# A new table of priority shifts for a list-scheduled six-stage decoder kernel

## The chip, the cores and the metric

The kernel runs on one core of one Trainium2 chip. The metric is device time in microseconds (us) from the first to the last instruction with what lies around them, the median of repeated runs.

## What is computed

Two layers of a decoder over 256 tokens of width 1024 in float32. Each layer is a feed-forward block, a mixer and a second feed-forward block, each followed by a layer norm of a weighted sum:

```python
def reference(x, positions, ...):
    h = x
    for layer in range(2):
        h = layer_norm(ALPHA * h + 0.5 * swiglu(h, ffn_w_in[layer, 0], ffn_w_out[layer, 0]), ...)
        if layer % 2 == 0:
            mix = hybrid_mixer(h, ...)       # gated delta rule + state-space scan
        else:
            mix = nsa_mixer(h, positions, ...)   # compressed, selected and window attention
        h = layer_norm(ALPHA * h + mix, ...)
        h = layer_norm(ALPHA * h + 0.5 * swiglu(h, ffn_w_in[layer, 1], ffn_w_out[layer, 1]), ...)
    return h

def swiglu(x, w_in, w_out):              # w_in 1024 x 5632, w_out 2816 x 1024
    gate, up = split(x @ w_in, 2)
    return (silu(gate) * up) @ w_out
```

The gated delta rule of the hybrid mixer solves a triangular system in each chunk of 64 tokens, for eight heads.

## The kernel before

The stages of the run are numbered 0 to 5: feed-forward, hybrid mixer, feed-forward, feed-forward, attention mixer, feed-forward. All weights are streamed from memory once.

**Products in three parts.** A float32 weight tile of 128 x 1024 lands in a buffer named `raw`. ScalarE (or VectorE) copies it, rounded, into `whi`; VectorE subtracts the two and keeps the rest in `wlo`. Activations are split in the same way (`x`, `g` or `gh` and `gl`, `fhi` and `flo` by their place). A product is then three matmuls: high by high, low by high, high by low. In most of a feed-forward stage, seven products of blocks stand for eight (`wide` in the code), which needs sums of weight blocks (`raw<-raw,raw` on VectorE), some of them made by accumulating transfers from GpSimd's queue.

**Turning.** The gated result of a chunk has to be transposed before the second product. In some chunks TensorE does that; in others ScalarE writes 16-bit `words`, SyncE issues two DMA transposes into `turned`, and ScalarE puts the result together (`gT`).

**Buffers.** Tiles of 128 x 1024 come from 44 slots shared by named streams (raw tiles, split tiles and so on), each with a quota. A stream's tiles are granted in program order. PSUM has eight banks under three names, `ps`, `mp` and `acc`.

**What sets the order.** The Python program first only records operations, 8,350 in all, each with its place in the program as its priority, and then runs a list scheduler (`Plan.order`). It walks in modelled time, and at every step takes, for the engine that can start soonest, the ready operation with the smallest priority. Costs, latencies, two DMA queues and the slots are modelled. The instructions are emitted in the order that comes out; each engine then works through its own list strictly in that order, waiting on semaphores for what isn't ready. SyncE's list holds most loads, the DMA transposes and the stores; GpSimd's list holds the accumulating loads.

**The table.** Before the scheduler runs, `SHIFTS` is applied: for each stage and engine it holds runs of (count, shift), counted over that engine's operations of the stage in program order. Operations past the last run get none:

```python
for eng, runs in shifts.items():
    mine = iter([op for op in ops if op.eng == eng])
    for count, shift in runs:
        for op in islice(mine, count):
            op.prio += shift
```

A shift of -500 lets an operation go ahead of ready operations that stand up to 500 places earlier. It can't make an operation ready sooner.

All instructions are recorded by one helper line (L707 in the profile), so tiles' names tell them apart.

Of the kernel before, what the change touches and what calls it, by code (L numbers as in the profile page):

```python
# [49 lines left out]

SHIFTS = {
    0: {
        "tensor": [(73, 35), (42, 0), (3, -303), (2, 677), (60, 285), (4, 0), (6, 272), (80, 180), (61, 0), (1, 89), (2, 0), (5, 76), (12, 0),
            (5, 185), (9, 128), (22, 0), (46, -94), (1, 272), (8, 0), (1, 429), (45, 247), (112, 0), (6, -69), (1, 1116), (147, 0), (19, -333)],
        "vector": [(26, 0), (11, 505), (3, 0), (1, 981), (9, 332), (2, 1157), (16, 37), (8, 0), (1, 36), (2, 12), (2, 0), (3, 40), (2, -49),
            (2, -314), (6, -28), (5, -335), (8, 0), (6, -130), (1, 239), (20, 0), (7, -457), (15, 90), (9, 68), (28, 27)],
        "scalar": [(51, 1316), (49, 299), (32, 0), (4, -174), (7, -332)],
        "sync": [(21, 512), (4, 0), (2, 1305), (42, -829), (1, -837)],
    },
    1: {  # L60
        "tensor": [(78, 0), (5, 102), (45, 13), (1, 126), (57, 0), (5, 165), (56, -1495), (2, 137), (46, 0), (1, 116), (27, 0), (2, 316), (4, 0),
# [4 lines left out]
        "vector": [(61, 79), (16, -214), (2, -277), (20, 0), (22, -481), (36, 0), (3, 243), (2, 0), (8, -1712), (6, 0), (3, 122), (3, 0), (2, -781),  # L66
            (1, 785), (7, 0), (5, -96), (13, 0), (3, -348), (12, 0), (5, 955), (6, 0), (2, -2056), (7, 82), (2, -244), (4, 0), (7, -2770), (2, -226),
            (7, -312), (14, -616), (13, 0), (2, -170), (3, 235), (31, 0), (1, 104), (3, 0), (45, -78), (11, -721)],
        "scalar": [(36, 0), (6, -475), (29, 0), (27, -175), (2, 128), (3, 0), (1, -552), (4, 68), (13, 0), (2, -580), (18, 0), (2, 1271), (31, 0),
            (26, -544), (51, 0), (2, 137), (15, 0), (11, 358), (8, -97), (2, 2193), (7, -854)],  # L70
        "gpsimd": [(3, 0), (2, -233)],
        "sync": [(40, 0), (1, -488), (4, 0), (4, -608)],
    },
    2: {
        "tensor": [(2, 151), (39, 28), (11, 0), (6, -515), (27, 0), (14, -125), (19, 120), (157, 30), (177, 0), (5, -87), (4, 0), (9, -961), (4, 0),
            (33, -162), (4, -408), (5, 100), (80, 0), (27, 151), (7, 0), (2, 167), (11, 0), (1, -218), (2, -189), (2, -136), (1, -210), (7, -310),
            (10, -171), (6, -305), (5, -340), (13, 61), (13, -822), (1, 0), (37, -386), (1, 98), (22, 0), (14, 68)],
        "vector": [(10, -109), (7, -190), (4, 103)],
        "scalar": [(12, 0), (3, -357), (78, 1148), (35, 0), (1, -118)],
    },  # L80
    3: {
        "tensor": [(36, 0), (4, -133), (4, 0), (6, -109), (1, 778), (37, 0), (2, 738), (31, 505), (107, 0), (7, 177), (18, 0), (23, 487), (5, 0),
            (2, 1186), (1, 1660), (23, 1445), (19, -442), (12, 41), (14, -333), (2, 0), (1, -306), (5, -732), (3, 0), (4, 101), (123, 0), (6, -597),
            (170, 0), (62, -115), (28, -595)],
        "vector": [(40, 239), (10, 0), (11, 402), (4, 1341), (5, 0), (1, 554), (110, 0), (6, -268)],
        "scalar": [(66, 735), (32, 0), (10, -856)],
        "sync": [(43, 0), (2, -897)],
    },
    4: {
        "tensor": [(1, 435), (72, 0), (8, 132), (1, 358), (38, 0), (19, 167), (1, 272), (10, 0), (7, 192), (1, 427), (14, -543), (8, 518), (68, 75),  # L90
            (60, 0), (7, -103), (5, 42), (70, 0), (122, 124), (3, 0), (4, -102), (3, 0), (1, -524), (10, -43), (3, -211), (17, 0), (8, -186),
            (2, -392), (2, 0), (36, -364), (1, -98), (2, -410), (9, 21), (39, 0), (10, 303), (17, 239)],
        "vector": [(68, 0), (3, -666), (71, 0), (9, -229), (3, 0), (25, -315)],
        "scalar": [(124, 98), (11, 0), (41, 123), (4, 0), (9, -109), (14, 5), (8, 0), (2, -850), (2, -72)],
        "sync": [(1, 31)],
    },
    5: {
        "tensor": [(51, 140), (26, 0), (2, 803), (90, 0), (23, 974), (14, 0), (17, 113), (5, 0), (89, 892), (47, 0), (4, 3124), (3, 3103), (1, 4070),
            (24, 937), (42, -1815), (2, 1390), (18, 0), (8, 322), (1, 0), (34, 288), (19, -2444), (14, -1291), (3, 0), (15, -1630), (12, -161),
            (2, 0), (125, -150), (5, 324), (4, 299), (18, 187), (21, 0), (14, 332), (4, 0), (28, 346)],  # L100
        "vector": [(12, 382), (19, 0), (4, 193), (20, 0), (18, 1029), (12, 0), (2, 1342), (6, 645), (12, 0), (79, -160)],
        "scalar": [(71, 853), (58, 53)],
        "sync": [(42, 0), (10, -188), (18, 98)],
    },
}

# [2469 lines left out]
```

## Time and profile before

| what | value |
|---|---|
| median of 3 runs | 1067.26 us (1066.71 to 1068.01) |
| profiled execution | 1069.88 us |
| its span | 1068.2 us |
| mean granted TensorE clock | 0.995 |
| TensorE matmuls busy | 1051.2 us, 98% |
| VectorE busy | 1004.6 us, 94% |
| ScalarE busy | 765.7 us, 72% |
| moved from memory | 221.30 MB, 208 GB/s over the span |

The span is the time from the first to the last instruction of the profiled execution; the time of that execution is measured around it. In rows, PE is TensorE's matmuls and PEld its weight loads, DVE is VectorE, ACT ScalarE, POOL GpSimd, and SPq SyncE's queue of transfers. Busy time counts an engine as busy from an instruction's start to its end; matmuls overlap in the pipeline and their ends are modelled.

### The profile page before, as it was taken

Reading aid. Unit: us, or ns where it says so; the run is one execution under the profiler, and the core shown is the slowest. Engines: PE = TensorE matmul, PEld = TensorE weight load, DVE = VectorE, ACT = ScalarE, POOL = GpSimd, SP = SyncE. Lnnn points to the kernel's source line nnn. Section 1 sums busy time; section 2 is a strip of 40 time slices with the busy share of each in tenths; the row PEclk is TensorE's granted clock in tenths of the full one; section 3 lists DMA queues with packets and bytes.
Section 4 is the critical chain, followed back from the end, with each engine's and each line's share of the span. In section 5 each row is a group of like instructions: output and inputs, shape, how many; then the busy total and the mean of one; then the engine's idle time right before and its main releaser. Section 6 shows DMA issues by size and latency. Waiting matters only on the chain.

```text
span 1068.2 us, 15981 instructions
## 1 busy us (share of the span) xinstructions
PE 1051.2 (98%) x5714; PEld 869.8 (81%) x5714; DVE 1004.6 (94%) x1417; ACT 765.7 (72%) x1154; POOL 88.5 (8%) x130
## 2 busy tenths in 40 slices
PE   9999999999999999999999999999999999999987
PEld 6877888899889888888888888888887778887866
DVE  7999999799989999998999999999988989999977
ACT  7677966479856977776876678788475867787771
POOL 1001000001000221100000200000011110000100
PEclk9999999999989999999999999999999999999999
DMA  9899996753772799889879846998563373687981
GB/s 316 277 286 263 257 322 196 200 144 102 180 200 84 209 272 333 238 239 263 273 228 318 222 158 211 263 260 267 169 204 132 112 234 80 198 249 199 274 271 40
DMA packets 178586, 233.52 MB, mean 219 GB/s; under 512 B 46973, under 2 KB 108106, under 8 KB 178506
## 3 DMA queue, kind: packets, MB, share of 16 engines
q1 hardware_dynamic: 169258, 214.67, 63.7%
q0 software_dynamic: 9248, 17.83, 9.9%
q8 instruction: 45, 0.74, 0.3%
q14 instruction: 35, 0.29, 0.1%
HBM read 221.30 MB, written 1.07 MB: 208 GB/s over the span
## 4 chain that ended last, share of the span: by engine, by line
PE 84%; DVE 7%; DMA 4%; ACT 2%; issue 1%; POOL 1%; SPq 0%; DVEq 0%; POOLq 0%; ACTq 0%
PE acc L707 33%; PE ps L707 26%; PE mp L707 25%; DMA raw<-in_ffn_w_in_dram 2%; DVE arena L707 1%; DMA raw<-in_ffn_w_out_dram 1%; DVE h L707 1%; DVE wlo L707 1%; DVE cv L707 1%; POOL arena L707 1%; DVE o L707 1%; ACT P L707 1%; DMA raw<-in_nsa_cmp_w_dram 1%; DVE F L707 0%; ACT sw L707 0%
## 5 line engine op out<-in xcount | busy, mean ns | idle before, releaser
L707 DVE TENSOR_TENSOR wlo<-raw,whi 128x1024 fp32r<-128x1024 f32 (+2 forms) x447 | 523.1, 1205 | 13.8 <-ACT whi L707 13.4
L707 ACT ACTIVATE whi<-raw 128x1024 fp32r<-128x1024 f32 (+2 forms) x426 | 424.9, 1046 | 66.9 <-DVE raw L707 37.8
L707 PE MATMUL ps<-whi,x 128*128 128x512 f32 (+1 forms) x544 | 146.0, 385 | 0.0
L707 DVE TENSOR_TENSOR raw<-raw,raw 128x1024 f32<-128x1024 f32 x94 | 112.1, 1216 | 2.6 <-DMA raw<-in_ffn_w_in_dram 2.1
L707 PEld LDWEIGHTS ps<-whi,x 128*128 128x128 f32 x544 | 97.6, 188 | 18.5 <-ACT vg L707 0.4
L707 PE MATMUL ps<-x,whi 128*128 128x512 f32 (+2 forms) x464 | 106.3, 344 | 0.5 <-ACT cv L707 0.5
L707 PE MATMUL acc<-wlo,gh 128*128 128x512 f32 x253 | 99.1, 392 | 1.7 <-DVE wlo L707 1.7
L707 PE MATMUL acc<-whi,gh 128*128 128x512 f32 x253 | 97.5, 393 | 1.5 <-ACT whi L707 1.5
L707 PE MATMUL acc<-whi,gl 128*128 128x512 f32 x253 | 97.7, 392 | 0.0
L707 PEld LDWEIGHTS ps<-x,whi 128*128 128x128 f32 (+1 forms) x464 | 78.2, 189 | 10.1 <-ACT cv L707 1.3
L707 PE MATMUL acc<-whi,x 128*128 128x512 f32 x256 | 82.2, 404 | 1.1 <-ACT whi L707 1.1
L707 PE MATMUL mp<-whi,x 128*128 128x512 f32 x288 | 78.9, 392 | 0.0
L707 PE MATMUL ps<-wlo,x 128*128 128x512 f32 (+1 forms) x272 | 78.2, 382 | 0.0
L707 PE MATMUL mp<-whi,fhi 128*128 128x512 f32 x192 | 75.0, 392 | 0.0
L707 PE MATMUL mp<-whi,flo 128*128 128x512 f32 x192 | 74.7, 390 | 0.0
L707 POOL DMA_DIRECT2D raw<-in_ffn_w_in_dram x34 | 41.1, 1209 | 382.3 <-DMA raw<-in_ffn_w_in_dram 142.1
L707 PE MATMUL ps<-x,wlo 128*128 128x256 f32 (+1 forms) x344 | 66.0, 284 | 0.0
L707 PE MATMUL acc<-whi,g 128*128 128x512 f32 x192 | 63.8, 391 | 0.0
L707 PEld LDWEIGHTS mp<-whi,x 128*128 128x128 f32 x288 | 53.1, 188 | 12.1 <-ACT vg L707 1.0
L707 PE MATMUL mp<-wlo,fhi 128*128 128x512 f32 x192 | 60.0, 392 | 1.8 <-DVE wlo L707 1.8
L707 PEld LDWEIGHTS acc<-wlo,gh 128*128 128x128 f32 x253 | 47.5, 188 | 12.7 <-DVE wlo L707 2.7
L707 PEld LDWEIGHTS acc<-whi,x 128*128 128x128 f32 x256 | 47.3, 188 | 12.5 <-ACT whi L707 1.7
(323 smaller groups left out, 1852.0 us busy)
## 6 DMA issues: line engine op xcount, KB each, us to landing
raw<-in_ffn_w_in_dram SPq DMA_DIRECT2D x162, 512.0 KB, 6.5
raw<-in_ffn_w_out_dram SPq DMA_DIRECT2D x88, 512.0 KB, 6.1
raw<-in_hyb_w_in_dram SPq DMA_DIRECT2D x44, 512.0 KB, 5.6
raw<-in_ffn_w_in_dram POOLq DMA_DIRECT2D x34, 512.0 KB, 9.5
raw<-in_ffn_w_in_dram SPq DMA_DIRECT2D x52, 256.0 KB, 4.5
raw<-in_hyb_w_out_dram SPq DMA_DIRECT2D x16, 512.0 KB, 4.4
raw<-in_nsa_w_in_dram SPq DMA_DIRECT2D x10, 512.0 KB, 5.1
raw<-in_nsa_cmp_w_dram SPq DMA_DIRECT2D x8, 512.0 KB, 4.9
```

Of the source, the lines that this page charges most:

```text
L707: r = getattr(getattr(nc, eng), fn)(*[res(a) for a in args], **{k: res(a) for k, a in kw.items()})
```

## The change

The table `SHIFTS` is replaced as a whole; nothing else is edited. By the description that came with it, the old and the new table are the outcome of a search, and the new one judged each order by the mean of replays in which transfers are issued when slots are free and land at scattered times. Runs that differ can be counted from the two tables and the program's list: of the tensor instructions, 479 of 812 in stage 0 get another shift, 916 of 1,375 in stage 1, 549 of 800 in stage 2, 568 of 792 in stage 3, 412 of 687 in stage 4 and 649 of 785 in stage 5. The last 18 SyncE entries of stage 5 are 12 loads of output weights, the two rows of the layer norm and the four stores; the entries 59 and 64 of that list are DMA transposes.

The diff, cut to the stages 3 and 5 (the others are rewritten in the same way):

```diff
--- before.py
+++ after.py
@@ -50,57 +50,60 @@
...
     3: {
-        "tensor": [(36, 0), (4, -133), (4, 0), (6, -109), (1, 778), (37, 0), (2, 738), (31, 505), (107, 0), (7, 177), (18, 0), (23, 487), (5, 0),
-            (2, 1186), (1, 1660), (23, 1445), (19, -442), (12, 41), (14, -333), (2, 0), (1, -306), (5, -732), (3, 0), (4, 101), (123, 0), (6, -597),
-            (170, 0), (62, -115), (28, -595)],
-        "vector": [(40, 239), (10, 0), (11, 402), (4, 1341), (5, 0), (1, 554), (110, 0), (6, -268)],
-        "scalar": [(66, 735), (32, 0), (10, -856)],
-        "sync": [(43, 0), (2, -897)],
+        "tensor": [(58, 217), (9, 0), (1, 99), (42, 0), (3, -97), (67, 0), (4, -120), (48, 667), (3, 0), (5, 851), (21, 0), (1, 372), (74, 89),
+            (24, 0), (84, 1255), (71, 0), (3, 388), (11, 0), (1, 531), (27, 0), (3, 397), (3, 0), (1, 405), (117, -629), (15, -906), (13, 0),
+            (3, -677), (13, 97), (29, 0), (11, 122), (6, 0), (12, 198)],
+        "vector": [(11, 237), (6, 0), (43, 175), (2, 816), (4, 727), (9, 637), (19, 0), (4, 1258), (18, 0), (1, 578), (4, 0), (6, 202), (33, 0),
+            (1, 77)],
+        "scalar": [(66, 487), (23, 0), (4, 446), (3, 162), (3, 0), (2, -331), (12, 0), (20, 658)],
     },
...
     5: {
-        "tensor": [(51, 140), (26, 0), (2, 803), (90, 0), (23, 974), (14, 0), (17, 113), (5, 0), (89, 892), (47, 0), (4, 3124), (3, 3103), (1, 4070),
-            (24, 937), (42, -1815), (2, 1390), (18, 0), (8, 322), (1, 0), (34, 288), (19, -2444), (14, -1291), (3, 0), (15, -1630), (12, -161),
-            (2, 0), (125, -150), (5, 324), (4, 299), (18, 187), (21, 0), (14, 332), (4, 0), (28, 346)],
-        "vector": [(12, 382), (19, 0), (4, 193), (20, 0), (18, 1029), (12, 0), (2, 1342), (6, 645), (12, 0), (79, -160)],
-        "scalar": [(71, 853), (58, 53)],
-        "sync": [(42, 0), (10, -188), (18, 98)],
+        "tensor": [(2, 197), (25, -123), (15, 0), (1, 769), (2, 0), (6, 64), (1, 0), (9, 299), (16, 0), (8, 1127), (38, -515), (45, 0), (2, 1282),
+            (16, -364), (1, 514), (19, 92), (81, 0), (1, 322), (61, 0), (3, 260), (5, 0), (2, 1081), (3, 0), (4, 3690), (16, 396), (10, 100),
+            (4, 4396), (29, 0), (14, 312), (2, -1131), (34, 0), (22, -910), (1, 65), (20, -455), (46, 120), (95, 0), (3, -282), (4, 0), (17, -146),
+            (36, 0), (15, -113), (2, 0), (1, -92)],
+        "vector": [(6, 580), (3, 0), (3, 163), (11, 0), (6, 65), (2, 0), (5, 114), (2, -89), (8, -768), (19, -95), (1, 732), (22, 404), (43, 0),
+            (8, -74), (10, 0), (3, -251), (5, 0), (27, -124)],
+        "scalar": [(8, 43), (9, -32), (46, 865), (30, 305), (25, 0), (4, 471), (2, 0), (1, 496)],
+        "sync": [(70, 0), (18, -517)],
     },
 }
```

## Rows read from the trace of the kernel before

**Rows 1.** From the profile page of the whole run: the span, busy time of the engines with their instruction counts, the busy share of the DMA engines in 40 slices (tenths), the shares of the chain that ended last, and the issues of output-weight loads with the median us from issue to landing.

```profile
span 1068.2 us, 15981 instructions
...
PE 1051.2 (98%) x5714; PEld 869.8 (81%) x5714; DVE 1004.6 (94%) x1417; ACT 765.7 (72%) x1154; POOL 88.5 (8%) x130
...
DMA  9899996753772799889879846998563373687981
...
PE 84%; DVE 7%; DMA 4%; ACT 2%; issue 1%; POOL 1%; SPq 0%; DVEq 0%; POOLq 0%; ACTq 0%
...
raw<-in_ffn_w_out_dram SPq DMA_DIRECT2D x88, 512.0 KB, 6.1
```

**Rows 2.** Stretches of 25 us, three from the middle feed-forward stages and one from the hybrid mixer: the stretch, its length, then busy time and instructions of each engine, the granted TensorE clock, the DMA share and GB/s.

```profile
500.00:525.00 25.00, 25.00 (x111) 20.51 (x110) 24.75 (x23) 19.74 (x22) 0.00 (x0) 1.00 0.86 243
650.00:675.00 25.00, 25.00 (x111) 20.63 (x110) 24.97 (x25) 21.55 (x25) 2.40 (x2) 1.00 0.83 268
700.00:725.00 25.00, 25.00 (x111) 20.53 (x110) 25.00 (x25) 20.35 (x24) 0.00 (x0) 1.00 0.94 271
300.00:325.00 25.00, 24.41 (x437) 22.42 (x436) 21.14 (x37) 11.22 (x17) 0.31 (x1) 0.86 0.50 156
```

**Rows 3.** The whole run cut into stages, with the same columns: the opening, the rest of the first feed-forward stage, the hybrid mixer, two feed-forward stages, the attention mixer, the last feed-forward stage, and the tail.

```profile
0.00:25.00 25.00, 22.84 (x94) 16.96 (x95) 17.02 (x25) 17.86 (x25) 4.61 (x25) 1.00 0.93 311
25.00:184.00 159.00, 157.62 (x718) 128.20 (x717) 155.08 (x167) 115.95 (x145) 10.78 (x9) 1.00 0.88 267
184.00:412.00 228.00, 226.73 (x1714) 198.96 (x1714) 211.30 (x429) 167.58 (x278) 20.19 (x28) 0.99 0.66 185
412.00:587.00 175.00, 175.00 (x805) 144.43 (x804) 170.55 (x187) 128.00 (x158) 13.82 (x13) 1.00 0.87 265
587.00:761.00 174.00, 174.00 (x796) 143.68 (x795) 173.40 (x208) 127.48 (x160) 9.95 (x10) 1.00 0.78 226
761.00:881.00 120.00, 118.78 (x792) 94.08 (x791) 106.90 (x213) 85.11 (x245) 16.16 (x36) 1.00 0.53 169
881.00:1050.00 169.00, 165.40 (x749) 134.35 (x749) 157.63 (x169) 123.72 (x150) 11.15 (x10) 1.00 0.72 201
1050.00:1068.20 18.20, 10.84 (x57) 9.16 (x55) 12.71 (x26) 0.00 (x0) 1.85 (x2) 0.86 0.16 59
```

**Rows 4.** TensorE's matmul side, who waited for whom over the whole run: total us, times, longest us.

```profile
PE acc L707 <- ACT whi L707: 2.6, 2, 1.5
PE mp L707 <- DVE wlo L707: 1.8, 2, 1.4
PE acc L707 <- DVE wlo L707: 1.7, 2, 0.9
```

**Rows 5.** TensorE's weight loads in order of time, those that sat idle before them (in brackets: idle us and what ended it), in the first and the last feed-forward stage: start us, us, engine, operation, out<-in, tile, count.

```profile
76.64 0.30 PEld L707 LDWEIGHTS mp<-wlo,fhi 128*128 128x128 f32 x2 [1.80 <-DVE wlo L707]
...
982.48 0.30 PEld L707 LDWEIGHTS mp<-wlo,fhi 128*128 128x128 f32 x2 [0.82 <-DVE wlo L707]
...
1021.72 0.19 PEld L707 LDWEIGHTS acc<-whi,gh 128*128 128x128 f32 x1 [1.95 <-ACT whi L707]
1022.98 0.19 PEld L707 LDWEIGHTS acc<-wlo,gh 128*128 128x128 f32 x1 [1.07 <-DVE wlo L707]
...
1029.71 0.19 PEld L707 LDWEIGHTS acc<-wlo,gh 128*128 128x128 f32 x1 [1.26 <-DVE wlo L707]
```

**Rows 6.** The chain that ended last, between 1008 and 1031 us: start us, us, what.

```profile
1012.76 10.53 DMA raw<-in_ffn_w_out_dram
...
1023.38 1.06 ACT whi L707
...
1028.44 1.23 DVE wlo L707
```

**Rows 7.** SyncE's queue between 1000 and 1026 us in order of time (start us, us over which the issues stretch, out<-in, count), then the same loads in a window that ends at 1013 us, and, as the last line, the duration of a transpose's issue over the whole run (ns, least/median/most).

```profile
1002.30 9.73 SPq L707 DMA_TRANSPOSE turned<-words  x2
1012.13 11.56 SPq L707 DMA_DIRECT2D raw<-in_ffn_w_out_dram  x10
...
1012.13 1.05 SPq L707 DMA_DIRECT2D raw<-in_ffn_w_out_dram  x2
...
L707 SPq DMA_TRANSPOSE turned<-words x32: 1232/1284/6093, 95.8 to 1008.5; - x32
```

**Rows 8.** Stretches around that place, columns as in rows 2 (the last two numbers are the DMA share and GB/s).

```profile
985.00:995.00 10.00, 10.00 (x46) 8.14 (x44) 9.97 (x9) 7.78 (x10) 1.20 (x1) 1.00 0.75 220
995.00:1002.30 7.30, 7.30 (x33) 5.83 (x32) 6.98 (x8) 6.38 (x8) 1.20 (x1) 1.00 1.04 257
1002.30:1012.10 9.80, 9.80 (x44) 8.01 (x44) 8.10 (x10) 6.30 (x7) 1.19 (x1) 1.00 1.09 321
1012.10:1023.30 11.20, 8.94 (x37) 6.56 (x37) 8.04 (x8) 5.28 (x5) 1.20 (x1) 1.00 1.23 227
```

**Rows 9.** The two conversions of a weight tile, all of their kind in the run: busy us, mean ns of one, idle time before them and what ended it.

```profile
L707 DVE TENSOR_TENSOR wlo<-raw,whi 128x1024 fp32r<-128x1024 f32 x436 | 514.6, 1215 | 13.0 <-ACT whi L707 12.6
L707 ACT ACTIVATE whi<-raw 128x1024 fp32r<-128x1024 f32 x416 | 417.9, 1053 | 61.0 <-DVE raw L707 37.8 <-DMA raw<-in_ffn_w_out_dram 5.4 <-DVE h L707 2.8
```

More of the change, by code (lines that the diff above doesn't have):

```diff
@@ L52 @@
     0: {
[L53 to L56, printed above, removed]
@@ L57 @@
-        "scalar": [(51, 1316), (49, 299), (32, 0), (4, -174), (7, -332)],
-        "sync": [(21, 512), (4, 0), (2, 1305), (42, -829), (1, -837)],
-    },
-    1: {
-        "tensor": [(78, 0), (5, 102), (45, 13), (1, 126), (57, 0), (5, 165), (56, -1495), (2, 137), (46, 0), (1, 116), (27, 0), (2, 316), (4, 0),
[4 rows of a table removed]
[L66 to L72, printed above, removed]
-    },
@@ L74 @@
-    2: {
[L75 to L79, printed above, removed]
-    },
@@ L89 @@
-    4: {
[L90 to L95, printed above, removed]
-    },
@@ L97 @@
-    5: {
-        "tensor": [(51, 140), (26, 0), (2, 803), (90, 0), (23, 974), (14, 0), (17, 113), (5, 0), (89, 892), (47, 0), (4, 3124), (3, 3103), (1, 4070),
-            (24, 937), (42, -1815), (2, 1390), (18, 0), (8, 322), (1, 0), (34, 288), (19, -2444), (14, -1291), (3, 0), (15, -1630), (12, -161),
-            (2, 0), (125, -150), (5, 324), (4, 299), (18, 187), (21, 0), (14, 332), (4, 0), (28, 346)],
-        "vector": [(12, 382), (19, 0), (4, 193), (20, 0), (18, 1029), (12, 0), (2, 1342), (6, 645), (12, 0), (79, -160)],
-        "scalar": [(71, 853), (58, 53)],
-        "sync": [(42, 0), (10, -188), (18, 98)],
+        "tensor": [(33, 160), (108, 0), (3, 677), (34, 0), (6, 297), (119, 81), (45, 0), (6, 674), (148, 0), (1, 496), (13, -172), (10, 272), (4, 0),
+            (7, 184), (2, 109), (29, 0), (4, 213), (2, 0), (10, 174), (2, 610), (15, 299), (4, 1187), (15, 382)],
@@ new lines @@
+        "vector": [(33, 0), (2, 157), (26, 0), (4, -268), (14, 337), (3, 0), (3, 569), (27, 137), (1, 118), (1, 188), (2, 0), (1, 274), (14, -404),
+            (2, 1222), (4, 0), (3, -1554), (1, -77), (2, -377)],
+        "scalar": [(130, 0), (1, 345), (11, 0), (1, 417)],
+        "sync": [(22, 73), (2, 63), (57, 57)],
+    },
+    1: {
+        "tensor": [(78, 0), (8, 108), (37, 0), (12, 87), (21, -126), (3, -45), (1, 0), (1, 57), (42, -4), (15, -78), (28, 28), (73, 0), (8, 274),
[5 rows of a table added]
+        "vector": [(77, 395), (7, 0), (11, 206), (1, 356), (71, 0), (3, -1139), (4, 0), (1, -443), (2, 62), (2, 462), (36, 0), (2, 257), (19, 146),
+            (10, 0), (1, 302), (5, -254), (20, 0), (9, -570), (12, 0), (1, -373), (4, -179), (3, 748), (1, -764), (21, 0), (2, -275), (22, 0),
+            (1, -191), (26, 0), (16, -3263)],
+        "scalar": [(103, 30), (21, 0), (40, 820), (90, 0), (1, -415), (2, 0), (11, -187), (17, 597)],
+        "gpsimd": [(7, 0), (1, 460)],
+    },
@@ new lines @@
+    2: {
+        "tensor": [(53, 0), (84, -29), (7, 325), (51, 0), (1, 267), (6, 0), (11, 149), (27, -808), (15, 57), (4, -369), (1, 0), (1, 298), (2, 177),
+            (28, 0), (37, -178), (40, 0), (1, 181), (1, 0), (1, 2273), (3, 2155), (2, 0), (2, 3273), (4, 118), (3, 2378), (107, 0), (26, 560),
+            (30, 0), (7, -157), (28, 0), (1, 1365), (6, 0), (2, 1935), (14, 0), (2, 1483), (48, 224), (64, 0), (9, -3469), (18, 0), (7, -571)],
+        "vector": [(27, 0), (3, 505), (33, -105), (9, -389), (46, 0), (18, -97), (4, -201), (1, 0), (2, -173), (2, -2013), (1, -172), (12, -1939)],
+        "scalar": [(101, 346), (7, 0), (2, 308)],
+    },
@@ new lines @@
+    4: {
+        "tensor": [(2, 381), (75, 0), (1, 134), (61, 0), (1, 245), (4, 0), (6, -264), (10, 115), (12, -208), (20, 48), (116, 0), (11, -736), (68, 0),
+            (4, 166), (21, 0), (19, 287), (20, 0), (6, -303), (1, 164), (19, 0), (1, 249), (2, 329), (7, 474), (12, 364), (13, 201), (12, 0),
+            (1, 286), (7, 0), (1, 367), (46, -238), (10, 0), (9, 228), (2, 0), (2, 686), (1, 356), (3, 0), (1, 292), (33, 0), (9, -596), (1, 1067),
+            (14, 0), (5, 761), (18, 150)],
+        "vector": [(68, 0), (10, -775), (14, 0), (8, 114), (67, 0), (12, 146)],
+        "scalar": [(98, 0), (12, -231), (17, 286), (9, 0), (1, 264), (18, 0), (6, 423), (20, 0), (2, 782)],
+        "gpsimd": [(64, 0), (7, -209)],
+        "sync": [(1, 107), (1, 75)],
+    },
```

9 rows, old and new, of the table SHIFTS are left out of this document.

## The prediction

> **What bounds the kernel.** I read the profile page first. TensorE is busy for 1051.2 of 1068.2 us, VectorE for 1004.6, and 84% of the chain that ended last is TensorE [rows 1]. The reader is to see that nothing but the matmul stream sets the length of most of the run, and that VectorE is close behind it. Whether that stream has slack inside is the next question, because busy time of pipelined matmuls can hide a slow pace. So I took 25 us stretches from the two middle feed-forward stages: each holds 111 matmuls and has no idle time [rows 2], that is 25.00 / 111 = 225 ns from one 128x512 product to the next. The same 111 comes back in three stretches 200 us apart, so this is the engine's own pace, and an order can't improve on it.
>
> The Trainium skill would have me look elsewhere: its page Perfetto Trace Analysis, section Identifying the Most-Contended Engine, says that matmul busy time is a poor measure of headroom and that the busy share of weight loads is a better one. That share is 81% here, which read as headroom would be about 200 us, against the 17 us that TensorE's idle time gives. The repeated pace of 111 products speaks for the smaller number, and I use it alone.
>
> The third view cuts the run by stage [rows 3]. Subtracting the busy from the length of each stretch gives TensorE's idle time: 2.16 us in the opening, 1.38 in the rest of the first feed-forward stage, 1.27 in the hybrid mixer, none in the two middle feed-forward stages (349 us together), 1.22 in the attention mixer, 3.60 in the last feed-forward stage up to 1050 us, and 7.36 in the tail. The sum is 16.99, which is all of 1068.2 - 1051.22. A new order of ready work can't shorten the opening (the first bytes have to come) nor much of the tail (two layer norms follow the last products). What an order can win is 1.38 + 1.27 + 1.22 + 3.60 = 7.5 us of idle time. Beside it stands a stretch in the hybrid mixer in which the granted clock falls to 0.86 in the mean over 25 us, after 437 small products [rows 2]; at half clock for 0.14 x 25 x 2 = 7 us, it costs about 3.5 us. The most that a perfect order could give back is therefore about 11 us, 1% of the run.
>
> **What the waits are.** TensorE's own waits are few and nearly all are for split weights: 2.6, 1.8 and 1.7 us [rows 4]. In time order they are a wait of 1.80 us on the weight side at 76.6 us, one of 0.82 at 982.5, and three of 1.95, 1.07 and 1.26 us between 1021.7 and 1029.7 [rows 5]. The last three have one cause, and the chain shows it: a transfer of output weights issued at 1012.76 lands 10.53 us later, its high part takes 1.06 us, a low part 1.23 [rows 6]. Such transfers land in 6.1 us in the median [rows 1]. It was late because the queue of SyncE was held for 9.73 us by two DMA transposes from 1002.30 on; ten output-weight loads were issued behind them, in 11.56 us [rows 7]. A transpose holds its queue for 1.28 us in the median and for 6.09 at most [rows 7]. The ten loads then meet a full memory path: the DMA share is 1.09 during the transposes and 1.23 in the stretch after [rows 8].
>
> **What the change does.** It adds, removes and resizes no instruction. It changes the number that is added to an operation's place in the program before the list scheduler picks among ready operations. Counted over the two tables, 3,573 of the 5,251 tensor instructions get another shift, at least 59% in every stage. So the order within an engine is drawn anew nearly everywhere, bounded by the dependences and by the buffers, which are still granted in program order. Direct cost in instructions: nothing. What moves is who waits.
>
> *Last feed-forward stage.* The last 18 SyncE entries go from no shift to -517: they are the 12 last output-weight loads, the two norm rows and the four stores. The transposes ahead of them lose their shift of +98 and stay at their place, some 820 and 860. So where a slot is free, these loads now sort ahead of the two transposes that held the queue, which they did not before. If they go first, the 10.53 us landing starts up to 9.7 us earlier and the three waits go: their idle time on TensorE is the stage's 3.60 less the wait at 982.5, about 2.8 us. If the slots come free only later (the planner grants them, and I can't see that in a trace), nothing is won. The bounds are 0 and 3.6. I take 2.8, since the first two of the loads leave within 1.05 us as soon as the second transpose is out [rows 7]; so the queue and not the buffers held these. What is late next: the transposes, whose turned tiles the last products but a few need; a transpose lands in 4.6 us in the median against products of 225 ns that are plentiful then, so I charge nothing, and up to 2 us if that cover is gone.
>
> The Trainium skill speaks against this term: DMA: Bandwidth & Descriptors, section Issuing engines are not separate DMA queues, says that all transfers end on the same 16 DMA engines and interleave. By that rule an earlier issue into a full path only moves the wait to its neighbour, and the term is 0. The trace agrees that the path is full from 995 us on, with its share of 1.04 to 1.23, but it also shows 0.75 in the 10 us before, which is room [rows 8].
>
> *First feed-forward stage.* One wait makes up the 1.38 us. The order around it is new; it goes or comes back elsewhere with like odds, so I take 0.7 won, bounds 0 and 1.4.
>
> *Mixers.* 2.49 us of idle time in 228 + 120 us, and the 3.5 us of slow clock, which comes while the small products of the triangular solve run, whatever stands around them. I take 1.0 won; the bounds are 6 won and 2.5 lost (the present idle time doubled).
>
> *Middle feed-forward stages.* They have no idle time and can only lose. VectorE is busy for 173.40 of 174.00 us in one and 170.55 of 175.00 in the other [rows 3], so a product pulled ahead of its split weights waits for one conversion of 1.05 us and one subtraction of 1.21 [rows 9]. I charge one such place as it showed in the first stage, 1.4 us; the bounds are 0 and two stages like the present last one, 7.2.
>
> **Sum.** -2.8 - 0.7 - 1.0 + 1.4 = -3.1 us. The profiled execution took 1069.88 us around its span of 1068.20, so it would go to 1066.8; it lies 2.6 us above the median of the three timed runs, 1067.26, and the same difference there gives **1064.2 us**. No change that can be told means within 0.2%, about 2.1 us: 1065.1 to 1069.4.
>
> **The rivals.**
>
> *The lateness only moves.* The loads are hidden or late in sum as before, because the path of the DMA engines is full around the place and the buffers are still granted in program order; the first three terms fall to -1.4 in sum and the new wait of 1.4 eats them: 1067.3. For it: share over 1.0 from 995 us on [rows 8]. Against it: 28 of the page's 40 slices show a DMA share of 8 tenths or less [rows 1]. This is also what comes out if the new table changes the planner's figures and not the chip's waits. The rule on the 16 engines, cited above, leads to this case. Chance 0.25.
>
> *VectorE becomes the bound of a middle stage (slower).* The place is the stage from 587 to 761 us, with 0.60 us of VectorE time to spare. If the new tensor order asks for weights in another sequence than VectorE splits them, VectorE idles once for its input and can't catch up; every us that it loses beyond 0.60 appears in the span. At a loss as large as the present last stage's, 3.6 us, in both middle stages and with nothing won: 1067.3 + 7.2 = 1074.5. It decides once VectorE idles some 3 us more between 412 and 761 us than the 5.05 that it does now, which would eat the whole sum. For it: both stages are at the floor already and 568 of 792 tensor shifts in the second one change. Against it: two thirds of VectorE's work there can be pulled ahead by as many slots as the buffers allow, and the present order, also one of many, keeps up. Chance 0.24.
>
> *The mixers gain too.* All of the 7.5 us and the slow clock go: 1067.3 - 11 = 1056.3. For it: 3.60 of the 7.5 us lie behind four waits only [rows 3, 5]. Against it: the solve's products are small in any order. Chance 0.08.
>
> **How the numbers follow.** My forecast, -3.1, has 0.43; with the larger gain 0.51 are faster, 0.25 within 0.2%, 0.24 slower. The predicted time is the likeliest case's, 1064.2. The range reaches from the best case, 1056, to two stages of lost VectorE time, 1074, which leaves out about 0.1 at either side. The likeliest case's own range is 1061 to 1066.
>
> **What would show it.** In the new profile TensorE's waits for whi and wlo should be under 3 us in all, where they are 6.1 now; the last stage's idle time up to 1050 us under 1 us; no transpose on SyncE near the end should hold the queue for 6 us with output-weight loads behind it; 111 products per 25 us should still fill the middle stages; the slow-clock stretch should be there still. I am wrong if the middle stages show idle time of more than 2 us on TensorE, if the span between the last weight load and the end grows, or if the waits of the attention mixer (probabilities from ScalarE, small tiles from VectorE) grow beyond their present 1.22 us.

## The result, and the profile of the changed kernel

The changed kernel takes 1061.05 us in the median of six executions (1059.18 to 1063.14), against 1068.59 us (1066.71 to 1072.31) for the kernel before in six executions on the same chip: a ratio of 0.9926, with a 95% interval from 0.9902 to 0.995. A second measurement gave 1062.62 against 1068.01, ratio 0.9955 [0.9932, 0.9979]. It is faster, by 0.5 to 0.7%, and the forecast of 1064.2 us asked for 0.3%.

The page of the changed kernel, line by line as in [rows 1]; its profiled execution took 1061.22 us, 1.8 us more than its span:

```profile
span 1059.4 us, 15975 instructions
...
PE 1046.3 (99%) x5714; PEld 871.8 (82%) x5714; DVE 1004.4 (95%) x1419; ACT 767.2 (72%) x1153; POOL 88.2 (8%) x127
...
PE 87%; DVE 9%; ACT 2%; issue 1%; DMA 1%; POOL 0%; SPq 0%; DVEq 0%; ACTq 0%
...
raw<-in_ffn_w_out_dram SPq DMA_DIRECT2D x88, 512.0 KB, 5.5
```

The span is 8.8 us shorter. TensorE's idle time went from 17.0 to 1059.4 - 1046.3 = 13.1 us, which is 3.9 of it. The other 4.9 us are busy time, 1051.2 before and 1046.3 now, for the same 5,714 matmuls. An order can't make a matmul cheaper; something made some of them dearer before, and that can't stand in the prediction's list of idle times; of it the prediction named only the slow clock, and expected it to stay.

The stages, cut where each layer norm ends (stretch, length, then busy time and instructions of TensorE's matmuls, its weight loads, VectorE, ScalarE and GpSimd, the granted clock, the DMA share and GB/s), and the tail:

```profile
0.00:190.30 190.30, 188.13 (x842) 153.65 (x843) 179.38 (x202) 135.09 (x172) 15.26 (x35) 1.00 0.88 275
190.30:416.70 226.40, 224.10 (x1715) 197.07 (x1714) 209.18 (x426) 174.66 (x285) 23.53 (x30) 1.00 0.67 188
416.70:589.70 173.00, 173.00 (x798) 143.31 (x797) 169.74 (x187) 125.13 (x152) 13.93 (x13) 1.00 0.86 260
589.70:762.60 172.90, 172.90 (x810) 144.02 (x809) 172.66 (x208) 127.66 (x160) 7.19 (x8) 1.00 0.78 232
762.60:886.10 123.50, 122.21 (x792) 96.13 (x791) 111.96 (x220) 87.13 (x245) 15.77 (x33) 1.00 0.50 160
886.10:1040.00 153.90, 153.90 (x704) 127.40 (x703) 148.10 (x155) 117.44 (x142) 10.63 (x9) 1.00 0.73 212
...
1040.00:1059.40 19.40, 12.10 (x62) 10.17 (x60) 13.39 (x27) 0.12 (x1) 1.85 (x2) 0.89 0.15 55
```

Against [rows 3] three things are new: the last feed-forward stage has no idle time up to 1040 us, the middle stages still have none, and the mean clock of the hybrid stage is 1.00 where it was 0.99. Some products moved over the borders of the stages, so lengths alone don't compare. For the table below each stage's products were charged at the pace that a quarter of their own kind keeps or beats in the kernel before, and this was taken off the stage's length; what is left is the time that the order costs. Both kernels were profiled twice (the second time as e8_changed_again and e11_before_again).

| stage | before, two profiles | changed, two profiles | difference of the means |
|---|---|---|---|
| 0 feed-forward, with the opening | 10.5, 9.8 us | 9.7, 9.5 us | -0.6 |
| 1 hybrid mixer | 26.1, 27.1 | 23.9, 24.5 | -2.4 |
| 2 and 3 feed-forward | 3.1, 3.6 | 2.5, 2.4 | -0.9 |
| 4 attention mixer | 23.5, 23.5 | 23.6, 23.7 | +0.1 |
| 5 feed-forward | 8.5, 7.5 | 3.2, 5.1 | -3.9 |

The sum, -7.7 us, is the difference of the mean spans (1060.45 and 1068.1). Two stages hold it: the last one, as forecast, and the hybrid mixer.

**The hybrid mixer: the clock.** Stretches of 4 us in the triangular solve, first of the kernel before:

```profile
300.00:304.00 4.00, 4.00 (x123) 3.64 (x122) 4.00 (x7) 3.69 (x5) 0.00 (x0) 1.00 1.06 316
304.00:308.00 4.00, 3.41 (x79) 3.36 (x76) 3.41 (x7) 1.43 (x2) 0.31 (x1) 0.69 0.93 312
308.00:312.00 4.00, 4.00 (x16) 2.70 (x13) 3.62 (x5) 0.04 (x1) 0.00 (x0) 0.50 0.21 78
312.00:316.00 4.00, 4.00 (x134) 4.00 (x134) 2.29 (x5) 1.36 (x2) 0.00 (x0) 0.96 0.01 4
```

and of the changed kernel:

```profile
300.00:304.00 4.00, 3.92 (x97) 3.58 (x94) 3.93 (x9) 2.36 (x4) 0.31 (x1) 1.00 0.81 257
304.00:308.00 4.00, 4.00 (x113) 3.78 (x111) 4.00 (x6) 0.42 (x1) 0.00 (x0) 1.00 0.04 10
308.00:312.00 4.00, 3.84 (x68) 3.58 (x65) 3.35 (x9) 1.72 (x3) 0.00 (x0) 1.00 0.42 131
```

Before, the clock is at half (1.2 GHz, a granted clock of 0.50) through 308 to 312 us, and 4 us of a busy TensorE do 16 products. By the clock's own records it is at half for 6.8 us, which costs 3.4. In the changed kernel it stays whole. The same record puts the start of the fall at 305.5 us. What stands there, by the matmuls in order of time (start us, us, operation, out<-in, tile, count), before:

```profile
300.50 1.82 PE L707 MATMUL acc<-T,Y 64*64 64x32 f32 x56
...
302.62 1.74 PE L707 MATMUL acc<-Y,T 64*64 64x32 f32 x53
304.94 0.24 PE L707 MATMUL acc<-Y,T 64*64 64x32 f32 x2 [0.59 <-issue]
...
305.03 3.31 PE L707 MATMUL acc<-X,AT 64*64 64x32 f32 x63
308.28 3.78 PE L707 MATMUL ps<-x,whi 128*128 128x512 f32 x8
```

and in the changed kernel:

```profile
292.61 2.28 PE L710 MATMUL acc<-X,AT 64*64 64x32 f32 x64
294.82 1.89 PE L710 MATMUL ps<-x,whi 128*128 128x512 f32 x7
...
296.86 2.05 PE L710 MATMUL acc<-T,Y 64*64 64x32 f32 x64
298.75 2.03 PE L710 MATMUL acc<-Y,T 64*64 64x32 f32 x64
300.87 2.05 PE L710 MATMUL acc<-X,AT 64*64 64x32 f32 x64
302.85 1.66 PE L710 MATMUL ps<-x,whi 128*128 128x512 f32 x6
...
309.00 2.07 PE L710 MATMUL acc<-X,AT 64*64 64x64 f32 x32 [0.16 <-DVE X L710]
```

Small products (64 x 64 by 32 or 64 columns) are as many, and here three groups of them run without a dense product (128 x 512) between them in both kernels. (Later in the solve the old order has four such groups in a row, the new one three.) What differs in these rows is a short gap: before, TensorE is idle for 0.59 us amid small products, and 0.6 us after the gap's end the clock falls; in the changed kernel the longest gap in the solve is 0.16 us. The second profile of the kernel before falls elsewhere in the solve, at 314.5 us, and again right behind a gap:

```profile
314.21 3.37 PE L707 MATMUL acc<-Y,T 64*64 64x64 f32 x32 [0.52 <-DVE Y L707]
```

The experiments' profiles say the same. The solve loses its clock for 6.8 us in six of the seven profiles with the old entries of stage 1 and without added products (both of the kernel before, e1, e2, e4, e7), each time 0.2 to 1.2 us after a gap of 0.48 to 0.63 us amid small products. It loses none in the five with the new entries, whose longest gap there is 0.17 us. The seventh is e6, with the same gap and a whole clock, so the gap alone doesn't decide:

```profile
303.61 0.24 PE L690 MATMUL acc<-Y,T 64*64 64x32 f32 x2 [0.53 <-issue]
```

Among dense products the kernel before has longer gaps, of 1.38 us at 75 us and 1.51 at 1020 us, and no fall behind them. The Trainium skill, TensorE: Matmul & The Clock Gate, section HAM oscillation, puts a falling clock down to TensorE idling for data between bursts. These rows agree that idle time stands ahead of the fall; here it is a short gap amid small products.

**The last stage: no wait.** TensorE's waits over the whole run (us in total, times, longest):

```profile
PE ps L710 <- DVE cv L710: 1.1, 1, 1.1
PE acc L710 <- POOL ones L710: 1.1, 1, 1.1
PE acc L710 <- ACT whi L710: 1.1, 1, 1.1
```

Of the 6.1 us for `whi` and `wlo` in [rows 4] there is 1.1 left, in the opening. (The second profile of the changed kernel has 1.2 us more, in the last stage.) SyncE's queue where it was held in [rows 7], and the stretches that answer to [rows 8]:

```profile
998.99 3.51 SPq L710 DMA_TRANSPOSE turned<-words  x1
1002.61 0.98 SPq L710 DMA_DIRECT2D raw<-in_ffn_w_out_dram  x2
1004.32 3.37 SPq L710 DMA_TRANSPOSE turned<-words  x1
1007.79 9.40 SPq L710 DMA_DIRECT2D raw<-in_ffn_w_out_dram  x8
```

```profile
995.00:1005.00 10.00, 10.00 (x46) 8.27 (x45) 9.46 (x10) 7.26 (x9) 1.19 (x1) 1.00 1.10 346
1005.00:1015.00 10.00, 10.00 (x46) 8.29 (x45) 9.97 (x10) 8.13 (x9) 1.20 (x1) 1.00 1.11 239
```

Two loads slip between the transposes; eight stay behind them. The DMA engines are as full as before. The wait is gone all the same, and whether the new SyncE entries did that is what the first experiments ask.

### The profile page after: what moved, and what is told of

Read it like the earlier page. It is cut to its first block, busy times and chain, and to the rows that moved or that the text cites. A ratio compares the mean times of both kernels' runs of the same rounds, so it can differ in the third digit from the quotient of the medians.

```text
span 1059.4 us, 15975 instructions
## 1 busy us (share of the span) xinstructions
PE 1046.3 (99%) x5714; PEld 871.8 (82%) x5714; DVE 1004.4 (95%) x1419; ACT 767.2 (72%) x1153; POOL 88.2 (8%) x127
## 4 chain that ended last, share of the span: by engine, by line
PE 87%; DVE 9%; ACT 2%; issue 1%; DMA 1%; POOL 0%; SPq 0%; DVEq 0%; ACTq 0%
PE acc L710 33%; PE ps L710 28%; PE mp L710 27%; DVE cv L710 2%; DVE wlo L710 2%; DVE arena L710 1%; DVE h L710 1%; POOL arena L710 0%; ACT P L710 0%; DMA raw<-in_ffn_w_in_dram 0%; DVE F L710 0%; DMA raw<-in_hyb_w_in_dram 0%; DVE o L710 0%; DVE X L710 0%; DVE sw L710 0%
## 5 line engine op out<-in xcount | busy, mean ns | idle before, releaser
L710 ACT ACTIVATE whi<-raw 128x1024 fp32r<-128x1024 f32 (+2 forms) x432 | 429.3, 1045 | 52.6 <-DVE raw L710 29.6
L710 PE MATMUL ps<-x,whi 128*128 128x512 f32 (+2 forms) x464 | 104.1, 338 | 1.9 <-DVE cv L710 1.1
L710 PEld LDWEIGHTS ps<-wlo,x 128*128 128x128 f32 x272 | 49.2, 188 | 8.4
```

The costliest lines, as they stand in the source:

```text
L710: r = getattr(getattr(nc, eng), fn)(*[res(a) for a in args], **{k: res(a) for k, a in kw.items()})
```

## The experiments

In the edits OLD and NEW stand for the two tables, by stage. Each ratio is to the kernel before, measured in the same series. A single execution of the kernel before lies anywhere from 1061.6 to 1078.0 us (87 of them, in three series), and its span goes with its granted clock: at 0.997 to 0.999 it is mostly 1060 to 1068 us, at 0.987 to 0.989 it is 1071 to 1076. So a second number stands beside most ratios. The time lost to the clock is (1 - granted clock) x span, the span rises by 0.84 to 1.03 us for each such us in the three series (fitted within each kernel, over all kernels of a series), and "at equal clock" is the difference to the kernel before with this taken out, with two standard errors.

### SyncE's new entries in the last stage alone

```diff
     5: {
...
-        "sync": [(42, 0), (10, -188), (18, 98)],
+        "sync": [(70, 0), (18, -517)],
```

> The old table with one entry of the new one: the SyncE shifts of stage 5, (70, 0), (18, -517). In SyncE's emitted list this puts two of the ten output-weight loads between the two transposes near the end and leaves the other eight behind the second; some 309 tensor instructions of stage 5 also change place. If the loads' place behind the transposes made the three late waits of the kernel before, those waits (4.3 us on the weight side) go and the time falls by about 2.8 us, a ratio of 0.997. If the new order of the computing engines made the gain, nothing is won: ratio 1.000 within 0.002, and the waits between the last transposes and the tail stay over 3 us.

1068.41 us, ratio 1.0002 [0.9976, 1.0028]; at equal clock -0.3 +- 0.9 us. Its queue has the changed kernel's order, a load pair between the transposes, and the transposes now take 1.25 and 2.57 us:

```profile
1008.22 1.25 SPq L690 DMA_TRANSPOSE turned<-words  x1
1009.57 1.01 SPq L690 DMA_DIRECT2D raw<-in_ffn_w_out_dram  x2
1011.94 2.57 SPq L690 DMA_TRANSPOSE turned<-words  x1
1014.62 7.90 SPq L690 DMA_DIRECT2D raw<-in_ffn_w_out_dram  x8
```

Its only wait on TensorE after 880 us is this one:

```profile
PE ps L690 <- ACT whi L690: 1.6, 1, 1.6
```

So two loads left earlier, as the prediction said, and the waits shrank: the kernel before has 3.6 us of them there, and 2.1 in its second profile. That is 0.5 to 2.0 us less waiting, and no more than 1.2 us of it can show in the time.

### The whole last stage alone

```diff
-SHIFTS = OLD
+SHIFTS = {**OLD, 5: NEW[5]}
```

> The old table with all of stage 5 from the new one. The last stage from its layer norm of stage 4 to its own took 5.6 us less in the changed kernel's profile. If that gain belongs to the stage's own table: 5.6 us won, ratio 0.995. If it came from the state in which the earlier stages left the buffers and the queues, less than half of it is won: ratio above 0.9975.

1068.06 us, 1.0006 [0.9976, 1.0035], at equal clock +0.7 +- 0.9 us. Behind the old stage 4 the new last stage wins nothing. In its profile TensorE waits 2.0 us for `whi` and 0.7 for another tile, and 1.0 us behind the first wait the clock is at half for 3.4 us, so this wait may have cost more than its own length.

### All stages but the last

```diff
-SHIFTS = OLD
+SHIFTS = {**NEW, 5: OLD[5]}
```

> The new table with stage 5 from the old one. By the layer norms of the two profiles, stages 0 to 4 are worth -1.3, -0.6, -1.8, -1.3 and +1.9 us, -3.1 in sum. If the stages' gains add: ratio 0.997, and the late waits of the last stage are back (over 3 us). If the gain of the whole is one of stage 5 alone: ratio 1.000. The half-clock stretch of 6.8 us in the hybrid mixer should be gone if it is the new order that removed it, and there at times if it is chance.

1065.91 us, 0.9976 [0.995, 1.0002]; one execution of twelve took 3240.10 us and isn't counted in the means. The mean time lost to the clock is 2.6 us, where the kernel before loses 5.9 in the same series; at equal clock -0.5 +- 1.0 us. What this kernel wins is the clock. It keeps the old last stage, and that stage's order costs 5.7 us here, less than in the kernel before (8.5 and 7.5); the expected waits of over 3 us didn't come back, there are 1.5.

### No DMA transposes at the end

```diff
-FLIP = [(0, 1, 1, 0), (0, 1, 1, 0), (1, 1, 1, 0), (1, 1, 1, 0)]
+FLIP = [(0, 1, 1, 0), (0, 1, 1, 0), (1, 1, 1, 0), (1, 1, 0, 0)]
```

The old table; in the last stage one chunk more is turned by TensorE, so that nothing holds the queue.

> The old table, but the chunk whose two DMA transposes held SyncE's queue near the end is turned by TensorE: 8 transposes of 128 x 128 on TensorE (about 0.9 us at 109 ns each) and no transpose on the queue ahead of the ten loads; the three ScalarE copies around the transposes go. If the hold of the queue made the loads late, the three waits (4.3 us) go and, with the 0.9 us paid, 2 us are won: ratio 0.998. If the memory path was simply full, the loads are as late as before and the time grows by 0.9 us: ratio 1.001.

1068.27 us, 1.0003 [0.9982, 1.0025], at equal clock -0.8 +- 0.9 us. After 880 us TensorE waits once, for 0.3 us. The wait is gone, and the expected 2 us aren't reached, 1.7 at most. With the 0.9 us that the eight transposes on TensorE cost by the estimate above, up to 2.6 us may have been won by the freed queue. The ten loads, and the longest wait of SyncE between 995 and 1030 us:

```profile
1005.96 17.98 SPq L690 DMA_DIRECT2D raw<-in_ffn_w_out_dram  x10
...
SPq L690 <- DVE raw L690: 7.9, 2, 6.0
```

Two loads leave 6 us earlier than in the kernel before, and one of those two is the load whose landing the chain of [rows 6] shows. The third, by the profile, waits 6.0 us for VectorE to be done with a `raw` tile and leaves at 1013.37 us; in the kernel before it left at 1013.28. The last leaves at 1023.6 us, and left at 1023.4. So the queue held the first two loads; without it, the next wait was for a buffer.

### The hybrid mixer's entries alone

```diff
-SHIFTS = OLD
+SHIFTS = {**OLD, 1: NEW[1]}
```

> The old table with the hybrid mixer's stage (1) from the new one. In 35 executions of the kernel before, the mean granted clock ran from 0.987 to 0.999 and the span rose by 0.86 us for each us of clock lost; the changed kernel's six executions show 0.997 to 0.999. Clock theory: the order of the mixer's small products is what the clock falls after, so this kernel shows 0.997 to 0.999 in nearly every execution and wins 3 us: ratio 0.997. Waits theory: the stage is worth its own 0.6 us and the clock's mean stays near 0.9945: ratio 0.9995.

1082.52 us, 1.0135 [1.0101, 1.017]: slower by 14.5 us. The solve keeps its clock, but TensorE runs out of work at the layer norm behind the mixer. Its longest wait, and two stretches at the place:

```profile
PE mp L689 <- DVE h L689: 10.9, 2, 10.7
```

```profile
410.00:420.00 10.00, 0.00 (x0) 0.00 (x0) 9.56 (x16) 0.34 (x1) 3.79 (x3) 0.72 1.11 282
420.00:430.00 10.00, 8.23 (x30) 6.31 (x31) 5.23 (x8) 2.76 (x5) 2.40 (x2) 0.60 0.96 273
```

```profile
420.67 1.94 PE L689 MATMUL mp<-ident,h 128*128 128x128 f32 x8 [10.74 <-DVE h L689]
```

For 10.74 us no product is ready: all of the mixer's are done and the next stage's input, `h`, isn't normed yet. In the kernel before and in the changed one, TensorE is busy for all of 400 to 430 us. The clock falls inside the gap, for 13.7 us by its records, of which 7.3 lie behind it and make running products dearer; at equal clock the kernel is 9.9 +- 2.0 us slower: the gap is most of the loss, the clock the rest.

### All stages but the hybrid mixer

```diff
-SHIFTS = OLD
+SHIFTS = {**NEW, 1: OLD[1]}
```

> The new table with the hybrid mixer's stage (1) from the old one. Clock theory: the falls come back (mean clock near 0.9945) and about 3.4 of the 7.5 us are lost again: ratio to the kernel before 0.996. Waits theory: only 0.6 us are lost, ratio 0.993, with the clock at 0.998.

1068.95 us, 1.0008 [0.9982, 1.0035]. The loss to the clock is back, 5.8 us in the mean (the kernel before: 5.4); at equal clock +0.9 +- 1.3 us. So more is lost than the 3.4 us expected for the clock: without the new entries of stage 1 nothing of the gain is left. Its profiled execution had a whole clock in the solve, at 0.998; its other eleven executions go from 0.998 down to 0.988. So the old order doesn't lose the clock each time, but in most executions. At the layer norm behind the mixer TensorE waits 2.3 us for `h`, which is part of the rest.

### The two last stages together

```diff
-SHIFTS = OLD
+SHIFTS = {**OLD, 4: NEW[4], 5: NEW[5]}
```

> The old table with stages 4 and 5 from the new one. Stage 5 alone won nothing; together with the new stages 0 to 4 it is worth 4.7 us. If it needs the state in which the new attention stage leaves queues and buffers: 3.7 us won, ratio 0.9965, with no long wait for weights in the last stage. If it needs the earlier stages, or the difference was one of chance in the landings: ratio above 0.999.

1066.34 us, 0.9987 [0.996, 1.0014], at equal clock -1.0 +- 1.3 us. No wait of TensorE is left after 880 us, and the order of the last stage costs 3.1 us, as in the changed kernel. e6, which has both new stages too, waits 0.3 us there; e2, with the new stage 5 alone, 2.7. So by the profiles that stage's shortening needs the new stages 4 and 5 together. In the time that is 2.3 us at most, less than the 3.7 expected.

### The changed kernel again

> The changed kernel again, beside the other three on the same chip. Ratio 0.9926 as before, within 0.003; mean clock 0.997 to 0.999; no wait for split weights over 1 us in the last stage.

1062.62 us, 0.9955 [0.9932, 0.9979]. Its profile has waits of 0.9 and 0.3 us for `whi` and `wlo` in the last stage, where the first had none. It loses 2.0 us to the clock in the mean of twelve executions, and the kernel before 5.4. With 1.03 us of span for each, that is 3.5 of the 5.3 us between the means; at equal clock -1.8 +- 1.4 us are left.

### Dense products put into the solve

In the kernel before, two 128 x 128 by 128 x 512 products are put ahead of three of the solve's groups of small products, six in all. Their sums land in a bank that the small products then overwrite; everything else keeps its order.

```diff
+    out = []
+    for o in order:
+        for op, bank, x in plan.dense:
+            if o[2] is op.args:
+                out += [("tensor", "matmul", (bank, x[0][:, 0, 0, :], ...), dict(start=True, stop=True))] * 2
+        out.append(o)
+    order = out
```

> The kernel before with its order kept and six products of 128x512 added on TensorE within the triangular solve: two ahead of each of three of its groups of 64 small products that ran without a dense product before them. Their results are overwritten by the small products. They cost 6 x 0.225 = 1.4 us. Clock theory, in the form that the run of small products is what the clock falls after: the mean clock rises from about 0.995 to 0.998 and 3.4 - 1.4 = 2 us are won, ratio 0.998. If the fall has another cause (the order of the other engines, the stretch before), the mean clock stays and the time grows by 1.4 us: ratio 1.0013.

1067.06 us, 0.9976 [0.9951, 1.0001]. The clock is at 0.998 in the mean of twelve executions, 0.996 at the least; the loss to it is 2.0 us, against 6.0 of the kernel before in the same series. At equal clock it is 1.5 +- 1.1 us slower, and six products at 225 ns are 1.35. The solve, in the same stretches:

```profile
304.00:308.00 4.00, 4.00 (x119) 3.59 (x117) 3.93 (x8) 2.11 (x2) 0.31 (x1) 1.00 0.94 290
308.00:312.00 4.00, 4.00 (x64) 3.26 (x62) 3.77 (x7) 0.42 (x1) 0.00 (x0) 1.00 0.31 120
```

This separates the clock from the table: more work, none of it useful, and the run gets no longer, because the clock stays up. It doesn't say which trait of the order matters. In this profile the gap of some 0.5 us is gone from the solve together with the fall. Only the middle pair of products stands between two groups of small ones (at 305.57 us, where the gap was); the other two pairs come straight behind eight dense products. And a run of 7.4 us of small products, from 310.71 us on, keeps the whole clock. A kernel with the gap closed and no dense product added was not run.

### The hybrid mixer and the stage behind it

```diff
-SHIFTS = OLD
+SHIFTS = {**OLD, 1: NEW[1], 2: NEW[2]}
```

> The old table with stages 1 and 2 from the new one. Stage 1 alone left TensorE idle for 10.7 us at the layer norm between the stages. If that is because the tables of the two neighbouring stages are drawn for each other, the idle time is gone here, and the clock's part is won: mean clock 0.998, ratio 0.997. If the new stage 1 needs the new stage 0 before it, the idle time of some 10 us is there again: ratio 1.013.

1065.82 us, 0.9968 [0.9945, 0.999]. No long wait at the layer norm; the loss to the clock is 1.8 us, and at equal clock the difference is +0.5 +- 1.1 us. The new entries of stage 2 are what the new entries of stage 1 lacked alone.

### The kernel before, profiled again

> The kernel before once more, for its trace. If the late waits in the last stage belong to its order, weights are waited for there for 4 us again; if they are chance of the landings, they differ by more than 2 us. A stretch at half clock of 6.8 us in the hybrid mixer, or none (mean clock 0.998), as in a part of the 64 executions so far.

One execution: 1069.68 us, span 1068.0. The clock falls again, 8 us later in the solve:

```profile
312.00:316.00 4.00, 3.48 (x49) 3.38 (x48) 2.98 (x7) 2.66 (x4) 0.00 (x0) 0.82 0.40 104
316.00:320.00 4.00, 4.00 (x26) 3.88 (x26) 2.40 (x3) 0.32 (x1) 0.00 (x0) 0.50 0.40 162
320.00:324.00 4.00, 4.00 (x30) 3.91 (x29) 2.62 (x6) 2.13 (x5) 0.00 (x0) 0.83 0.00 0
```

and the waits after 891 us are 2.1 us where the first profile had 3.6:

```profile
PE acc L707 <- DVE wlo L707: 1.7, 2, 0.9
PE ps L707 <- ACT whi L707: 0.4, 1, 0.4
```

So the fall is likely with this order, and its place and the size of the last stage's waits vary from one execution to the next.

## Why the prediction was right, and where it was not

The direction was right and the sum too small. In part that was luck: the largest single piece of the gain is the clock, which the prediction expected to stay as it was, and of the queue, its largest term, less came than it took. Step by step:

- **The middle stages: right in their floor, wrong in the charge.** 25 us hold 112 products in each of the three stretches of [rows 2] (111 before), and TensorE has no idle time. The 1.4 us charged for a new wait did not come. VectorE has 172.90 - 172.66 = 0.24 us to spare in the second of these stages, less than before, and the rival that it becomes the bound did not happen.
- **The first stage: about right.** 0.7 taken; the wait at 76.6 us is gone, and the stage's order costs 0.6 us less.
- **The last stage: right in the profile, wrong in its mechanism.** 2.8 taken. (The 2.8 takes a weight-side wait of 0.82 us off TensorE's idle time of 3.60; on the matmul side that wait is 0.39 and the other three 3.2.) The waits are gone or down to 1.2 us and the order costs 3.9 us less in the profiles. But the cause named, loads held behind transposes, was put right in part in e1 and taken away in e4, and the time changed by -0.3 +- 0.9 and -0.8 +- 0.9 us. The step that failed is "the queue and not the buffers held these": it holds for the first two of the ten loads only, and with the queue free the third waited 6.0 us for a buffer (e4). No more than some 1.2 us (e1) can have been won by the new SyncE entries alone. What shortens the stage is the new order of stages 4 and 5 together (e7), and of this -1.0 +- 1.3 us shows in the time. The rival that the lateness only moves described these single edits; it does not describe the changed kernel.
- **The mixers: the term that was mis-sized.** 1.0 taken, "the slow-clock stretch should be there still". It is not. The prediction saw the 3.5 us and took them for a property of the small products "whatever stands around them" (of the 437 that it calls small, 384 are). What stands around them matters: e9 keeps the order and adds dense products, and the loss falls from 6.0 to 2.0 us; the new entries of stage 1 do the same (e3, e10) and the old ones bring it back (e6). Whether it is the dense products or the short gap amid the small ones that counts is open. The clock is 3.5 us of the gain in e8's series, two thirds of it. The rival that the mixers gain too, at a chance of 0.08, is the one that had this in it. Beside this the stage costs 1.0 us more than before: 3.4 us come from the clock and 1.0 goes back, which leaves the 2.4 of the table.
- **What was said would show it.** Waits for `whi` and `wlo` under 3 us: 1.1, and 2.2 in the second profile. Idle time of the last stage under 1 us: none up to 1040 us, and 1.2 in the second profile. No transpose that holds the queue for 6 us with loads behind it: right, 3.51 and 3.37 us, though eight loads still stand behind the second. The time from the end of the last weight load's issue to the end of the run not grown: right, 44.5 us before and 42.2 now. Attention mixer's waits not above 1.22 us: 123.50 - 122.21 = 1.29, just above it. Slow clock still there: wrong.

The sum with its true terms, by the two pairs of profiles: -3.9 (last stage), -3.4 +1.0 (hybrid mixer), -0.6 (first), -0.9 (middle), +0.1 (attention) = -7.7 us. Over all executions of e8's series it is -5.3: -3.5 from the clock and -1.8 +- 1.4 from the rest. The two agree on the clock and not on the rest. In the first measurement the medians are 7.5 us apart, near the profiles' figure, and its interval and e8's overlap. Why the last stage's 3.9 us in four profiles are not found whole in e8's times stays open: its waits differ between two executions of one kernel by 1.5 us, and two profiles of each are few.

Open is also where the executions at a clock of 0.987 to 0.989 lose theirs. They lose 12 to 14 us, more than one fall of 6.8 us at half and the tail explain, and none of them was profiled. (e2's profiled execution, at 0.993, shows one such further place: the 3.4 us at half behind its wait in the last stage.)

The table was replaced as one piece, and the runs show that its pieces lean on each other. The new entries of the hybrid mixer alone cost 1.35%, with stage 2 they win 0.3%; the new last stage is shorter only behind the new stage 4. No kernel tried was faster than the changed one.

## What to carry to other kernels

Read the granted clock beside idle time, and treat a fall of it in a run of small products as something that the order of work can remove: here a new order without the short gaps, and the old order with six dense products put in, both kept it whole. Look for a gap ahead of the fall, however short. A wait that a queue explains well may be worth less than its length, since a buffer may be the next thing to wait for; free the queue alone, and look at the time and not only at the wait. Entries of a schedule that meet at a border, such as a layer norm, are drawn for each other, and swapping one side alone can cost more than the whole is worth.

## What the runs showed of the hardware

TensorE's clock went to half in the triangular solve 0.2 to 1.2 us after a gap of 0.48 to 0.63 us amid small products, and stayed there for 6.8 us while TensorE was busy: in six profiles, two of them of the kernel before, from 305.5 and from 314.5 us on. One profile with such a gap kept its clock (e6), and gaps of up to 1.51 us among dense products were followed by no fall in the kernel before. In the last stage of e2 a gap of 2.0 us and in that of e5 two gaps of 0.9 and 0.8 us were, with 3.4 us at half each time. Six dense products of 128 x 512 were enough to stop it, with the mean clock going from about 0.994 to 0.998; the gap went too, so which of the two it took is not shown. The scatter of a kernel on one core, here from 1061.6 to 1078.0 us, goes with the granted clock of the execution (correlation 0.85 to 0.93), so kernels that differ by some 3 us are better compared at equal clock beside their medians, unless the change acts on the clock itself.
